# Computing adaLN modulation vectors: standing weight tiles on TensorE in one layer, row sums on VectorE in the other

## The chip, the cores and the metric

The kernel runs on one core of a Trainium2 chip. The metric is the device time in microseconds (us), and the lower the better; one execution was also recorded with the hardware profiler.

## The reference

Two trunk layers run over 256 context tokens and 1024 latent tokens of width 1024. Each layer has a mixing part (four kinds of two-direction chunked scans, then an output projection) and a channel part (a squared-ReLU MLP of width 4096). Both parts begin with a normalisation that is scaled and shifted by modulation vectors, and end in a residual addition with a gate. The change is in how these vectors are computed. Cut to that:

```
for layer in range(DEPTH):
    mod_l = silu(c) @ w_ada[layer] + b_ada[layer]        # latent tokens
    mod_c = silu(c_ctx) @ w_ada[layer] + b_ada[layer]    # context tokens
    sh1, sc1, g1, sh2, sc2, g2 = split(mod, 6)           # each 1024 long
    h = rmsnorm(x) * (1 + sc1) + sh1
    x = x + g1 * (mixers(h) @ w_out)
    h = rmsnorm(x) * (1 + sc2) + sh2
    x = x + g2 * (relu(h @ w1) ** 2 @ w2)
```

`w_ada` is 1024 x 6144 in each layer, 25 MB of 32-bit numbers. It is multiplied by two vectors only, one for the context and one for the latent tokens, so this is a matrix-vector product that sits beside large matrix products. The 6144 columns are cut into three thirds of 2048, numbered r = 0, 1, 2: the first holds sh1 and sc1, the second g1 and sh2, the third sc2 and g2.

## The kernel before, in words

Activations lie with features on the 128 partitions and tokens along the row, in token blocks of 256, 512 and 512. Every large product runs in a split precision: each operand is held as a high and a low part, and `mm3` (L293, L294, L295) issues three matmuls for one 128 x 128 block of weights. `whalf` loads 256 KB of raw weights on the SyncE queue (L280), makes the high part on ScalarE (L281) and the low part on VectorE (L282).

The program runs in this order for each layer: the mixers, the output projection, the MLP. The first third of the first layer's modulation (`ada_unit`) comes ahead of everything. The order on each engine is that of the Python program, rearranged at build time by a scheduler of the framework; on the chip each engine works through its list in that order and waits at an instruction that isn't ready.

**Mixers.** Scan work comes from generators (`mix_vec` and others), which put small matmuls on TensorE with VectorE and ScalarE work between them: L990 prepares operands on VectorE for the matmuls of L1018, L955 multiplies with two moving columns, L1043 copies on ScalarE what L833 multiplies. Dense projections are put between them as filler by the class `Fill`. A step of it is six matmuls of `mm3`, so that a projection of 128 columns over one token block has four steps; then an evacuation function reads the PSUM bank (L741 and others on VectorE). Dense blocks take their PSUM banks from a ring of three, `self.dbanks = Ring((0, 1, 2))`.

`Fill.also` is a second generator, advanced at some of the filler's steps. In the first layer it computes thirds 1 and 2 of that layer's modulation, by `ada_part` with pieces of W = 256 columns. For each of eight blocks of 128 rows, `ada_part` loads a tile (L402), multiplies it by the block's element of c for each of the two tokens and adds it to an accumulator (L406 for the first block, L408 for the others). After the eighth, a matmul with one column of ones (L413) sums each 128 columns of the accumulator over the partitions, and L419 adds the bias:

```
for k in range(NK):
    w = wring.next()(W)
    nc.sync.dma_start(w, self.io["w_ada"][l, r, k, :, g, h:h + W])
    for i, j in enumerate(toks):
        c = self.cc[:, k, j:j + 1]
        ...
            nc.vector.scalar_tensor_tensor(A[i], w, c, A[i], op0=ALU.mult, op1=ALU.add)
    yield
...
        nc.tensor.matmul(ps[...], lhsT=A[i][:, 128 * cb:128 * cb + 128], rhs=one, ...)
```

That is 144 yields in the first layer, at three of five steps. About 250 steps of the filler are left when `also` is set.

**MLP of the first layer.** The second layer's modulation is computed here, by the same `ada_part` with W = 512: third 0 for both tokens, thirds 1 and 2 for the latent token alone. The function `filler` advances it after each of the 32 blocks of hidden features. PSUM banks come from a ring of eight; L525 adds the output to the residual on VectorE, reading PSUM.

The matmuls of the modulation have plain 32-bit operands, and TensorE runs each of them as two instructions.

Of the kernel before, what the change touches and what calls it, by code (L numbers as in the profile page):

```python
# [156 lines left out]
class Fill:  # L157
# [10 lines left out]
    def step(self):  # L168
        while self.q:
# [3 lines left out]
            for cost in gen:  # L173
                self.n += 1
                if self.also and self.n % 5 in (0, 2, 4):
                    next(self.also, None)
                return cost
# [20 lines left out]
class K:  # L198
    def __init__(self, ctx, tc, io):
# [16 lines left out]
        self.d_a = dp.tile([2, 4, NC], F32, name="d_a")  # L216

# [98 lines left out]
    def params(self, tmp):  # L316
# [5 lines left out]
        nc.vector.tensor_tensor(c2, c2, b, op=ALU.mult)  # L322

# [67 lines left out]
    def ada_part(self, l, r, toks, wring, tmp, acc, banks, W):  # L391
# [3 lines left out]
        one = self.m64[:, 1:2]  # L395
        nt, nb = len(toks), W // 128
        for q in range(2048 // W):
            g, h = divmod(q * W, 512)
            A = [b(W) for b in acc[:nt]]
            for k in range(NK):  # L400
                w = wring.next()(W)
                nc.sync.dma_start(w, self.io["w_ada"][l, r, k, :, g, h:h + W])  # L402
                for i, j in enumerate(toks):
                    c = self.cc[:, k, j:j + 1]
                    if k == 0:
                        nc.vector.tensor_scalar(A[i], w, c, None, op0=ALU.mult)  # L406
                    else:
                        nc.vector.scalar_tensor_tensor(A[i], w, c, A[i], op0=ALU.mult, op1=ALU.add)  # L408
                yield
            ps = self.bank(banks().next())  # L410
            for i in range(nt):
                for cb in range(nb):
                    nc.tensor.matmul(ps[:, 2 * cb + i:2 * cb + i + 1], lhsT=A[i][:, 128 * cb:128 * cb + 128], rhs=one,  # L413
                                     start=True, stop=True)
            o = 16 * r + nb * q
            mo = self.mod[:, l, o:o + nb, toks[0]:toks[0] + nt]
            bb = self.bada[:, l, o:o + nb].unsqueeze(2).to_broadcast([128, nb, nt])
            v = ps[:, 0:2 * nb].rearrange("p (c j) -> p c j", j=2)[:, :, 0:nt]
            nc.vector.tensor_tensor(mo, v, bb, op=ALU.add)  # L419
            if (r == 0 and g >= 2) or (r == 2 and g < 2):  # L420
                nc.vector.tensor_scalar(mo, mo, 1.0, None, op0=ALU.add)
            yield
# [1315 lines left out]
```

## Time and profile before

| | |
|---|---|
| median of 3 timed runs | 3307.71 us (3307.68 to 3312.28) |
| the profiled execution's own time | 3300.05 us |
| its span, first to last instruction | 3298.2 us |
| TensorE (PE) busy | 3215.6 us, 97% |
| VectorE (DVE) busy | 2121.8 us, 64% |
| ScalarE (ACT) busy | 1286.1 us, 39% |
| mean granted TensorE clock | 0.992 of full speed |
| moved by DMA | 278.85 MB, 85 GB/s on the mean |

Stretches of the span are given in us from its start. The first layer's mixers end at about 790, its output projection at about 900, its MLP at about 1800; then the second layer follows. PE stands for TensorE's matmuls, PEld for its weight loads, DVE for VectorE, ACT for ScalarE, SP for SyncE. Busy time of a group is the union of its instructions where they overlap one another, and the mean is that of one instruction from start to end, so that a pipelined instruction costs less than its mean.

### The profile page before, as it was taken

The page shows a single profiled execution, that of the slowest core. Times are in us where ns is not written, and L with a number is a line of the kernel's source. Part 1 is how long each engine was busy: PE and PEld are TensorE (multiplying, and loading weights), DVE is VectorE, ACT ScalarE, POOL GpSimd, SP SyncE. Part 2 cuts the span into 40 slices and gives each one's busy share as a digit, 9 for nine tenths or more (in the row PEclk, how much of TensorE's full clock was granted, in tenths as well). Part 3 has the DMA queues.
Part 4 walks back from the last instruction along what each step waited for, and adds up shares of the span by engine and source line. Part 5 has one row for each costly group of instructions (what it writes and reads, how often), then busy time and mean ns, then how long its engine had stood idle before and what let it go on. Part 6 is the DMA issues. An engine that isn't in the chain of part 4 may idle for free.

```text
span 3298.2 us, 52930 instructions
## 1 busy us (share of the span) xinstructions
PE 3215.6 (97%) x20936; PEld 2640.0 (80%) x20936; DVE 2121.8 (64%) x4218; ACT 1286.1 (39%) x2665; POOL 10.8 (0%) x41
## 2 busy tenths in 40 slices
PE   7998899999999999999999999999999999999998
PEld 4786688877888888888888678788778888888887
DVE  4778887787666656555655586866756555554546
ACT  4665565445322122121212565765445322222222
POOL 0000000000000000000000000000000000000000
PEclk9999899999999999999999999999999999999999
DMA  5113444434322222222211222333315111111111
GB/s 206 61 50 127 122 133 148 121 101 146 103 80 71 83 65 80 69 64 64 77 39 34 76 66 77 110 114 109 103 58 163 53 50 46 51 51 46 51 48 65
DMA packets 175010, 278.85 MB, mean 85 GB/s; under 512 B 21097, under 2 KB 66825, under 8 KB 174505
## 3 DMA queue, kind: packets, MB, share of 16 engines
q1 hardware_dynamic: 173464, 273.66, 26.5%
q8 instruction: 164, 2.69, 0.3%
q10 hardware_dynamic: 1296, 1.81, 0.2%
q14 instruction: 86, 0.70, 0.1%
HBM read 229.75 MB, written 45.64 MB: 83 GB/s over the span
## 4 chain that ended last, share of the span: by engine, by line
PE 88%; DVE 5%; DMA 3%; ACT 3%; issue 1%; SPq 0%; DVEq 0%; ACTq 0%
PE psum L293 23%; PE psum L294 23%; PE psum L295 23%; PE psum L830 2%; PE psum L600 2%; PE psum L631 2%; PE psum L633 2%; PE psum L632 1%; PE psum L817 1%; PE psum L833 1%; PE psum L1018 1%; PE psum L705 1%; PE psum L1357 1%; PE psum L413 1%; DVE px L990 1%
## 5 line engine op out<-in xcount | busy, mean ns | idle before, releaser
L525 DVE SCALAR_TENSOR_TENSOR x<-psum,st,x 128x512 f32<-128x512 f32 (+1 forms) x648 | 441.3, 690 | 213.2 <-PE psum L295 212.3
L281 ACT ACTIVATE pc<-st 128x512 fp32r<-128x512 f32 x256 | 161.2, 632 | 847.5 <-PE psum L294 808.7
L294 PE MATMUL psum<-pc,pc 128*128 128x512 f32 (+1 forms) x1296 | 475.9, 367 | 0.0
L293 PE MATMUL psum<-pc,pc 128*128 128x512 f32 (+1 forms) x1296 | 475.8, 367 | 0.0
L295 PE MATMUL psum<-pc,pc 128*128 128x512 f32 (+1 forms) x1296 | 473.8, 366 | 0.0
L293 PE MATMUL psum<-Hhi,pc 128*128 128x512 f32 (+1 forms) x1280 | 471.9, 369 | 1.7 <-ACT pc L281 1.5
L294 PE MATMUL psum<-Hlo,pc 128*128 128x512 f32 (+1 forms) x1280 | 471.9, 369 | 0.1
L295 PE MATMUL psum<-Hhi,pc 128*128 128x512 f32 (+1 forms) x1280 | 470.5, 368 | 0.0
L293 PE MATMUL psum<-Hhi,pw 128*128 128x512 f32 (+1 forms) x1192 | 451.0, 379 | 5.7 <-ACT pw L281 2.5
L295 PE MATMUL psum<-Hhi,pw 128*128 128x512 f32 (+1 forms) x1192 | 445.2, 374 | 0.0
L294 PE MATMUL psum<-Hlo,pw 128*128 128x512 f32 (+1 forms) x1192 | 444.8, 373 | 0.0
L504 DVE TENSOR_TENSOR st<-st 128x256 f32<-128x256 f32 (+1 forms) x160 | 101.8, 637 | 301.8 <-ACT pc L503 300.7
L293 PEld LDWEIGHTS psum<-pc,pc 128*128 128x128 f32 x1296 | 244.4, 189 | 43.8 <-DVE x L525 1.3
L295 PEld LDWEIGHTS psum<-pc,pc 128*128 128x128 f32 x1296 | 244.0, 188 | 43.0 <-issue 2.7
L294 PEld LDWEIGHTS psum<-pc,pc 128*128 128x128 f32 x1296 | 244.5, 189 | 41.3 <-issue 2.1
L293 PEld LDWEIGHTS psum<-Hhi,pc 128*128 128x128 f32 x1280 | 241.2, 189 | 43.5 <-ACT pc L281 2.4
L294 PEld LDWEIGHTS psum<-Hlo,pc 128*128 128x128 f32 x1280 | 241.3, 189 | 40.9 <-DVE Hlo L481 0.5
L295 PEld LDWEIGHTS psum<-Hhi,pc 128*128 128x128 f32 x1280 | 241.1, 188 | 40.9 <-DVE pc L282 0.6
L293 PEld LDWEIGHTS psum<-Hhi,pw 128*128 128x128 f32 x1192 | 226.7, 190 | 51.4 <-issue 10.1
L282 DVE TENSOR_TENSOR pc<-st,pc 128x512 fp32r<-128x512 f32 x256 | 175.5, 690 | 137.9 <-ACT pc L281 117.3
L295 PEld LDWEIGHTS psum<-Hhi,pw 128*128 128x128 f32 x1192 | 226.2, 190 | 37.6 <-issue 2.1
L294 PEld LDWEIGHTS psum<-Hlo,pw 128*128 128x128 f32 x1192 | 226.8, 190 | 36.2 <-issue 2.2
(398 smaller groups left out, 4950.4 us busy)
## 6 DMA issues: line engine op xcount, KB each, us to landing
st<-w_ff SPq DMA_DIRECT2D x256, 256.0 KB
st<-w_inT SPq DMA_DIRECT2D x96, 256.0 KB
ph<-w_ada SPq DMA_DIRECT2D x128, 128.0 KB
st<-w_out SPq DMA_DIRECT2D x50, 256.0 KB
pc<-w_ada SPq DMA_DIRECT2D x48, 256.0 KB
st<-w_ada SPq DMA_DIRECT2D x48, 256.0 KB
d_z<-st SPq DMA_DIRECT2D x40, 256.0 KB
ps<-w_ada SPq DMA_DIRECT2D x32, 256.0 KB
```

The lines of the kernel that those rows point to most:

```text
L281: nc.scalar.activation(hi, raw, AF.Copy)
L282: (eng or nc.vector).tensor_tensor(lo, raw, F(hi), op=ALU.subtract)
L293: t.matmul(out, lhsT=w[0], rhs=m[0], start=first, stop=False)
L294: t.matmul(out, lhsT=w[0], rhs=m[1], start=False, stop=False)
L295: t.matmul(out, lhsT=w[1], rhs=m[0], start=False, stop=last)
L413: nc.tensor.matmul(ps[:, 2 * cb + i:2 * cb + i + 1], lhsT=A[i][:, 128 * cb:128 * cb + 128], rhs=one, start=True, stop=True)
L504: nc.vector.tensor_tensor(r, r, r, op=ALU.mult)
L525: nc.vector.scalar_tensor_tensor(x, ps, self.mod[:, l, 40 + o, j:j + 1], x, op0=ALU.mult, op1=ALU.add)
L600: t.matmul(ps[:, 0:304], lhsT=h[a], rhs=u[b], start=(k + i == 0), stop=(k == NK - 1 and i == 2))
L631: t.matmul(ps[:, e, :], lhsT=h[0], rhs=u[0], start=(k == 0), stop=False)
L633: t.matmul(ps[:, e, :], lhsT=h[1], rhs=u[0], start=False, stop=(k == NK - 1))
L830: nc.tensor.matmul(o, lhsT=ST[r0:r0 + kd, c, d, :], rhs=qd[d](c)[r0:r0 + kd, :], start=(j == 0), stop=False, tile_position=(r0, 0))
```

## The change

First layer, thirds 1 and 2 (`ada_tiles`): for each of the 32 blocks of 128 output columns, eight 128 x 128 blocks of `w_ada` are loaded as two tiles of 512 words, each block stands as TensorE's weights, and the two tokens' c are the two moving columns. The eight products add up in PSUM, and one VectorE instruction adds the bias. Three tile buffers replace four tiles and two accumulators; the generator is advanced at every seventh step of the filler.

Second layer (`ada_rows`): the weights are stored transposed, so that an output column's 1024 weights lie along a row. A half row of c is loaded into all 128 partitions (from a copy in device memory, `d_c`, written at the start on GpSimd's queue), and one VectorE instruction multiplies a 128 x 512 tile with it and sums each row. The two halves are added, then the bias. TensorE takes no part. The rows go through five buffers, c through one; `filler` advances it by three yields of two tiles each. For third 0 the tiles are loaded once for each token.

The arrays of weights are laid out on the host for this: `w_adaW` for the first layer, `w_adaR` for the second.

```
--- before.py
+++ after.py
@@ -172,7 +172,7 @@
                 self.q[1].pre(self.slots - self.q[0].n)
             for cost in gen:
                 self.n += 1
-                if self.also and self.n % 5 in (0, 2, 4):
+                if self.also and self.n % 7 == 0:
                     next(self.also, None)
                 return cost
             self.q.pop(0)
@@ -214,6 +214,7 @@
         self.d_b = dp.tile([4, 128, NT], F32, name="d_b")
         self.d_v = dp.tile([128, NC, 260], F32, name="d_v")
         self.d_a = dp.tile([2, 4, NC], F32, name="d_a")
+        self.d_c = dp.tile([2, 1024], F32, name="d_c")
 
 
     @staticmethod
@@ -320,6 +321,8 @@
         self.logsig(b, c2, a)
         nc.scalar.activation(b, b, AF.Exp)
         nc.vector.tensor_tensor(c2, c2, b, op=ALU.mult)
+        for j in range(2):
+            nc.gpsimd.dma_start(self.d_c[j].rearrange("(k p) -> p k", p=128), self.cc[:, :, j])
 
     def params2(self, tmp):
@@ -388,36 +391,43 @@
             m = self.mod[:, l, a:a + 8, :]
             nc.vector.tensor_scalar(m, m, 1.0, None, op0=ALU.add)
 
-    def ada_part(self, l, r, toks, wring, tmp, acc, banks, W):
-
-
-        nc = self.nc
-        one = self.m64[:, 1:2]
-        nt, nb = len(toks), W // 128
-        for q in range(2048 // W):
-            g, h = divmod(q * W, 512)
-            A = [b(W) for b in acc[:nt]]
-            for k in range(NK):
-                w = wring.next()(W)
-                nc.sync.dma_start(w, self.io["w_ada"][l, r, k, :, g, h:h + W])
-                for i, j in enumerate(toks):
-                    c = self.cc[:, k, j:j + 1]
-                    if k == 0:
-                        nc.vector.tensor_scalar(A[i], w, c, None, op0=ALU.mult)
-                    else:
-                        nc.vector.scalar_tensor_tensor(A[i], w, c, A[i], op0=ALU.mult, op1=ALU.add)
+    def ada_tiles(self, l, rs, wring, banks, queue):
+
+
+        nc = self.nc
+        for r in rs:
+            for o in range(16):
+                ps = self.bank(banks().next())[:, 0:2]
+                for h in range(2):
+                    w = wring.next()(4, 128)
+                    queue.dma_start(w, self.io["w_adaW"][r - rs[0], o, :, 4 * h:4 * h + 4, :])
+                    for k in range(4):
+                        nc.tensor.matmul(ps, lhsT=w[:, k, :], rhs=self.cc[:, 4 * h + k, 0:2], start=(h + k == 0), stop=(h * k == 3))
+                c = 16 * r + o
+                one = 1.0 if r == 2 and o < 8 else 0.0
+                nc.vector.tensor_scalar(self.mod[:, l, c, :], ps, self.bada[:, l, c:c + 1], one, op0=ALU.add, op1=ALU.add)
                 yield
-            ps = self.bank(banks().next())
-            for i in range(nt):
-                for cb in range(nb):
-                    nc.tensor.matmul(ps[:, 2 * cb + i:2 * cb + i + 1], lhsT=A[i][:, 128 * cb:128 * cb + 128], rhs=one,
-                                     start=True, stop=True)
-            o = 16 * r + nb * q
-            mo = self.mod[:, l, o:o + nb, toks[0]:toks[0] + nt]
-            bb = self.bada[:, l, o:o + nb].unsqueeze(2).to_broadcast([128, nb, nt])
-            v = ps[:, 0:2 * nb].rearrange("p (c j) -> p c j", j=2)[:, :, 0:nt]
-            nc.vector.tensor_tensor(mo, v, bb, op=ALU.add)
-            if (r == 0 and g >= 2) or (r == 2 and g < 2):
+
+    def ada_rows(self, l, r, toks, wring, cs, queue):
+
+
+        nc = self.nc
+        S = self.mod[:, 1 - l, 0:16, :]
+        for j in toks:
+            for h in range(2):
+                c = cs.next()(512)
+                queue.dma_start(c, self.d_c[j:j + 1, 512 * h:512 * h + 512].to_broadcast([128, 512]))
+                for o in range(16):
+                    w = wring.next()(512)
+                    queue.dma_start(w, self.io["w_adaR"][r, o, :, 512 * h:512 * h + 512])
+                    nc.vector.scalar_tensor_tensor(w, w, 1.0, c, op0=ALU.mult, op1=ALU.mult, accum_out=S[:, o:o + 1, h])
+                    if o % 2:
+                        yield
+            mo = self.mod[:, l, 16 * r:16 * r + 16, j]
+            nc.vector.tensor_tensor(mo, S[:, :, 0], S[:, :, 1], op=ALU.add)
+            nc.vector.tensor_tensor(mo, mo, self.bada[:, l, 16 * r:16 * r + 16], op=ALU.add)
+            if r in (0, 2):
+                mo = self.mod[:, l, 16 * r + (8 if r == 0 else 0):16 * r + (16 if r == 0 else 8), j]
                 nc.vector.tensor_scalar(mo, mo, 1.0, None, op0=ALU.add)
             yield
@@ -1455,7 +1465,7 @@
 
         ao = hp.alloc(1536, True) if l == 0 else None
         if l == 0:
-            fill.also = ada([ao.sub(256 * i, 256) for i in range(6)], lambda: self.dbanks)
+            fill.also = ada([ao.sub(512 * i, 512) for i in range(3)])
         self.feat_hg(hg[0])
         share(hg[0], hg[1], "V")
         fill.add(*(self.gate(6 + p, GLG + p, True) for p in range(2)))
@@ -1591,9 +1601,8 @@
         tbs = TBS if l == 0 else TBS[1:]
         b.mix_open(l)
 
-        def ada(bufs, banks):
-            for r in (1, 2):
-                yield from b.ada_part(0, r, (0, 1), Ring(bufs[:4]), None, bufs[4:6], banks, 256)
+        def ada(bufs):
+            return b.ada_tiles(0, (1, 2), Ring(bufs), lambda: b.dbanks, nc.sync)
         b.mixers(l, ada)
         b.outproj(l)
         na = 3
@@ -1604,12 +1613,12 @@
         aring = Ring(zip(cs[nw + nf::2], cs[nw + nf + 1::2]))
         def ada1(bufs, l=l):
             for r in range(3) if l == 0 else ():
-                yield from b.ada_part(1, r, (0, 1) if r == 0 else (1,), Ring(bufs[:4]), None, bufs[4:6], lambda: b.banks, 512)
+                yield from b.ada_rows(1, r, (0, 1) if r == 0 else (1,), Ring(bufs[:5]), Ring(bufs[5:]), nc.sync)
         tmps = b.tmps
         gen = ada1(cs[nw:nw + nf] + tmps.items[4:])
 
         def filler():
-            for _ in range(4):
+            for _ in range(3):
                 next(gen, None)
         if l == 0:
             b.tmps = Ring(tmps.items[:4])
@@ -1705,7 +1714,9 @@
     for d in range(2):
         ga[:, 16 * d:16 * d + 16, d, :] = gla_w_a[:, d]
     A["gla_w"] = ga
-    A["w_ada"] = ca(w_ada.reshape(2, 8, 128, 3, 4, 512).transpose(0, 3, 1, 2, 4, 5))
+    A["w_ada"] = ca(w_ada[:1, :, :2048].reshape(1, 8, 128, 1, 4, 512).transpose(0, 3, 1, 2, 4, 5))
+    A["w_adaW"] = ca(w_ada[0, :, 2048:].reshape(8, 128, 2, 16, 128).transpose(2, 3, 1, 0, 4))
+    A["w_adaR"] = ca(w_ada[1].T.reshape(3, 16, 128, 1024))
     at = _cols()
     seg = lambda n: w_in[:, :, at[n][0]:at[n][1]]
     iff = seg("ml_if").reshape(2, 1024, 2, 2, 4)
```

## Rows read from the trace of the kernel before

**Rows 1.** Busy table of the page: busy us, share of the span, instructions.

```profile
span 3298.2 us, 52930 instructions
...
PE 3215.6 (97%) x20936; PEld 2640.0 (80%) x20936; DVE 2121.8 (64%) x4218; ACT 1286.1 (39%) x2665; POOL 10.8 (0%) x41
```

**Rows 2.** Chain that ended last, of the page: shares by engine.

```profile
PE 88%; DVE 5%; DMA 3%; ACT 3%; issue 1%; SPq 0%; DVEq 0%; ACTq 0%
```

**Rows 3.** Windows: stretch, length, busy PE, PEld, DVE, ACT, POOL; granted clock, DMA.

```profile
250.00:300.00 50.00, 47.15 (x401) 34.94 (x400) 38.27 (x114) 34.60 (x96) 0.00 (x0) 1.00 0.45 143
300.00:400.00 100.00, 77.96 (x738) 61.90 (x737) 84.78 (x193) 57.08 (x111) 0.00 (x0) 0.85 0.36 111
400.00:800.00 400.00, 396.83 (x3221) 325.95 (x3220) 319.50 (x827) 198.92 (x497) 1.53 (x14) 1.00 0.40 120
1000.00:1700.00 700.00, 700.00 (x3703) 604.15 (x3702) 410.10 (x673) 144.32 (x254) 0.00 (x0) 1.00 0.23 70
1950.00:2450.00 500.00, 491.32 (x4562) 397.78 (x4560) 361.15 (x818) 292.56 (x661) 1.60 (x14) 1.00 0.31 97
```

**Rows 4.** Windows, finer, the stretches with a granted clock below 1.

```profile
310.00:330.00 20.00, 10.66 (x126) 8.64 (x127) 17.40 (x40) 7.41 (x14) 0.00 (x0) 0.66 0.26 86
360.00:400.00 40.00, 34.85 (x303) 28.31 (x304) 30.74 (x74) 20.49 (x41) 0.00 (x0) 0.79 0.46 139
```

**Rows 5.** Waits of PE, 290 to 790: total us, times, longest.

```profile
PE psum L1018 <- DVE px L990: 9.8, 4, 4.6
PE psum L833 <- ACT px L1043: 5.5, 4, 3.0
PE psum L413 <- DVE ph L408: 3.5, 1, 3.5
PE psum L293 <- DVE st L741: 2.3, 1, 2.3
```

**Rows 6.** Line L413: count, ns min/median/max, first and last start, by layer.

```profile
L413 PE MATMUL psum<-st,ph x128: 164/250/353, 292.9 to 763.1; 128*128 128x1 f32 x128
...
L413 PE MATMUL psum<-st x128: 164/250/250, 1005.2 to 1682.3; 128*128 128x1 f32 x128
```

**Rows 7.** Timeline of PE around one burst: start, us, instruction.

```profile
1005.21 1.84 PE L413 MATMUL psum<-st 128*128 128x1 f32 x16
1006.91 0.37 PE L293 MATMUL psum<-Hhi,pc 128*128 128x256 f32 x1
1007.12 0.28 PE L294 MATMUL psum<-Hlo,pc 128*128 128x256 f32 x1
1007.24 0.28 PE L295 MATMUL psum<-Hhi,pc 128*128 128x256 f32 x1
```

**Rows 8.** Timeline of PE around matmuls with two moving columns.

```profile
335.40 0.95 PE L955 MATMUL psum<-st,px 128*128 128x2 f32 x8
336.21 0.48 PE L295 MATMUL psum<-Hhi,pw 128*128 128x512 f32 x1
336.52 0.39 PE L293 MATMUL psum<-Hhi,pw 128*128 128x512 f32 x1
336.75 0.40 PE L294 MATMUL psum<-Hlo,pw 128*128 128x512 f32 x1
```

**Rows 9.** DVE groups, 216 to 790, then 900 to 1750: busy us, mean ns.

```profile
L408 DVE SCALAR_TENSOR_TENSOR ph<-ph,st 128x256 f32<-128x256 f32 x224 | 99.7, 479 | 0.2 <-DMA ph<-w_ada 0.2
...
L406 DVE TENSOR_SCALAR ph<-ph,st 128x256 f32<-128x256 f32 x32 | 10.7, 347 | 4.2 <-PE psum L413 4.2
...
L408 DVE SCALAR_TENSOR_TENSOR st<-st 128x512 f32<-128x512 f32 x64 | 46.8, 747 | 3.0 <-DMA st<-w_ada 2.9
```

**Rows 10.** Line L419: count, ns min/median/max, first and last start.

```profile
L419 DVE TENSOR_TENSOR st<-psum,st x28: 156/164/171, 295.3 to 1682.5; 128x4 f32<-128x4 f32 x24, 128x8 f32<-128x8 f32 x4
```

**Rows 11.** Windows of line L408, then of L406, 300 to 400.

```profile
300.00:400.00 100.00, 17.92 (x40) 0.85 0.36 111
...
300.00:400.00 100.00, 1.22 (x4) 0.85 0.36 111
```

**Rows 12.** DMA queue, 100 to 110: packets, MB, share of 16 engines.

```profile
q1 hardware_dynamic: 110, 0.00, 0.6%
```

## The prediction

> **What bounds the kernel now.** I read the busy table first: TensorE is busy for 3215.6 of 3298.2 us [rows 1], so the reader should see an engine with 83 us of idle time in the whole span. Busy time alone proves little, so next comes the chain of work that ended last: 88% of it is TensorE, 5% VectorE [rows 2]. A change can thus gain in two ways only: less TensorE work, or fewer of those idle microseconds.
>
> The windows view says where they lie [rows 3]. In the first layer's MLP (1000 to 1700 us) TensorE is busy for all 700 us; VectorE does the second layer's modulation there at 410 of 700, and nothing waits for it. In the first layer's mixers TensorE idles for 2.9 us in 250 to 300, 22.0 us in 300 to 400 and 3.2 us in 400 to 800: 28.1 us together. In the second of these VectorE is busy for 85%, and the granted clock is 0.85. Cut finer [rows 4], the clock falls to 0.66 and 0.79 just where TensorE has been idle. The clock has two levels, 2.4 and 1.2 GHz, so a mean c says that 2(1-c) of the time ran at half speed, and a busy time b holds about (1-c)b lost: 0.34 x 10.7 + 0.21 x 34.9 = 10.9 us, an estimate. What the mixers lose is so about 28 + 11 = 39 us. The waits view names the releasers: VectorE (L990, L413's own accumulators, L741) and one ScalarE copy [rows 5].
>
> The second layer's mixers run the same code without modulation work. From 1950 to 2450 they idle for 8.7 us in 500 at full clock with VectorE at 72% [rows 3]. That is the yardstick for the first layer once VectorE is relieved.
>
> **The change, part by part.**
>
> *TensorE's added work.* A matmul with 32-bit operands runs as two records: 64 of L413 in each layer show as 128 [rows 6]. The price of a burst comes from the starts around it. Sixteen records with one moving column start at 1005.21; the second matmul after them starts at 1007.12; 0.12 of that is the ordinary step of the 256-column matmuls: 1.79 us, 0.111 a record, change of operand type included [rows 7]. Two moving columns are not dearer: eight records of L955 take 336.52 - 335.40 - 0.23 = 0.89 us, again 0.111 [rows 8]. The weights are what costs. Added: 2 thirds x 16 columns x 8 blocks = 256 matmuls, 512 records, 56.8 us, as 32 bursts of 1.78 us. Removed: 128 records in the first layer, 14.2 us, and 128 in the second layer's part, 14.2 us. TensorE's account: +56.8 - 28.4 = +28.4 us. The 14.2 us of the MLP are a sure gain, as that stage has no idle time to hide them; the mixers get +42.6.
>
> Here a page of the Trainium skill can be weighed. The row shows 0.111 us for a record with one or two columns. "TensorE: Matmul & The Clock Gate", section "Back-to-back issue gap", gives some 60 cycles for an isolated matmul of 1 to 64 columns, about 25 ns at full clock. By that figure the account would be 256 x 0.025 = +6.4 us in place of +28.4; the measurement decides, and it goes with the weight loads.
>
> *VectorE's relief in the mixers.* Gone are 224 multiply-adds, 99.7 us, and 32 multiplies, 10.7 us [rows 9]; the 16 additions of bias become 32 at 0.16 us [rows 10], 2.6 us more. In 300 to 400 the relief is 17.9 + 1.2 = 19.1 us [rows 11] of the 84.8.
>
> *How much of the 39 us comes back.* In 300 to 400 TensorE's own work without waits and slow clock is 78.0 - 10.9 = 67.1; less 24 old records (2.7) it is 64.4. The old bursts lie between 292.9 and 763.1 [rows 6] with 15 steps of the filler to each (9 yields at 3 of 5); that makes about 2.1 us a step, so 7 steps are 14.6 us: 6.8 bursts in this stretch, 12.1 us, and TensorE needs 76.5. VectorE then has 84.8 - 19.1 + 1 = 67. So VectorE stops being the longer of the two. Bounds: nothing comes back if the gaps are latency alone; all 33 (22.0 + 10.9) comes back if TensorE simply becomes the limit. I leave 8 of it: the 5.5 us behind the ScalarE copies of L1043 [rows 5], which VectorE's load does not make, and about 2 us per 100 as in the second layer. So 25 come back here. Of the 6 us in the other stretches I count 1. Together 26 us, bounds 15 and 39.
>
> *VectorE in the MLP.* 112 multiply-adds and 16 multiplies of 512 elements become 128 row sums of 512 elements. The multiply-add costs 747 ns [rows 9]; no row shows one that also sums along its row. Between 0.75 and twice that, VectorE gains between about 6 and 102 us of work in a stage where it idles for 290 of 700, and TensorE never waits [rows 3]. I cost it at nothing. The cover is that idle time and the ring of eight banks; if it were gone, the weight splits behind it (L282) would be late.
>
> *Transfers.* In the mixers 128 loads of 128 KB become 64 of 256 KB, the same bytes. A tile's buffer is freed at least one burst, some 15 us, before its next use, so its load is early; but now it is TensorE, in order, and not VectorE that stands behind a late one, with the dense work queued behind. In the MLP 96 loads become 128, with 8 loads of a repeated half row of c through one buffer: the SyncE queue waits there for sixteen sums, and the weight loads behind it wait too; with TensorE at no idle in 700 us I count nothing. The two stores of c at the start are 2048 elements of 4 bytes on GpSimd's queue, while the DMA engines feed the start. The nearest row: 110 tiny packets take 0.6% of 16 engines' 10 us, 8.7 ns each [rows 12]; 2048 of them over 16 engines are 1.1 us. Bounds 0 and 3; I take +1.
>
> *Sum.* +28.4 - 26 + 1 = +3.4 us. Against the profiled execution: span 3298.2 to 3301.6, time 3300.05 to 3303.5. The median of the timed runs, 3307.71, lies 7.7 above that execution; I put the same 3.4 on it: 3311.1.
>
> **The rivals.**
>
> *The gaps are latency (slower).* VectorE's work is mixed finely with the scan's, and the chain from ScalarE to VectorE to TensorE may be long whatever the load. Then only about 15 to 18 of the 39 return: 28.4 - 16.5 + 1 = +13, 3321. For it: L1018's waits for L990 are single waits of up to 4.6 us [rows 5]. Against it: the second layer runs that chain at 8.7 us in 500. It decides from the point where less than 23 us return.
>
> *Banks of the filler (slower).* The dense work and the bursts share a ring of three PSUM banks. A burst every 7 steps and a dense block of 4 steps mean that nearly every third turn is a burst's, so that dense work alternates between two banks and must wait until VectorE has read the one before. A wait of this kind is in the trace once, 2.3 us (L293 for L741) [rows 5]. At a third of the 32 bursts it is 25 us on top of the sum: +28, 3336. It decides from three such waits on. Against it: a freer VectorE reads sooner.
>
> *All comes back (faster).* The bursts fall into TensorE's gaps and the clock stays up: 28.4 + 1 - 38 = -8.6, 3299. It needs 36 of 39 us; a stretch as clean as 400 to 800, at 3.2 us in 400 [rows 3], speaks for it.
>
> *The page's issue gap holds (faster).* If the weight loads of consecutive bursts hid each other, the account would be +6.4 and the sum 6.4 - 26 + 1 = -18.6, 3289. The rows measure 0.111 with the same operand shapes, so I give it under 1 in 50.
>
> *Row sums hold up the MLP (slower).* The 14.2 us are given back: +18, 3326. TensorE's 700 of 700 speaks against it.
>
> **How the numbers follow.** The forecast (22 to 35 us return, nothing new waits) has 0.45 and reaches from -5.6 to +7.4 us, 3302 to 3315. Latency 0.23, banks 0.11, row sums 0.04: slower together 0.38. All back 0.15 and the issue gap 0.02: faster 0.17. A measurement of this kernel tells about 0.2%, 6.6 us, from no change; the cases fall on these bounds nearly as they stand. The time is that of the forecast, 3311. The range takes in the rival with everything back (3299) and the latency rival with some waits at the banks, to +20 (3328).
>
> **What would show it.** Right: 512 records of the new matmul line between about 220 and 760 us at 0.111 each; VectorE near 67 of 100 in the stretch from 300, the clock back near 1.00 there, idle time of TensorE in 250 to 800 under 12 us; the first layer's mixers ending some 17 us later (42.6 - 26), its MLP 14 us shorter, everything after the same. Wrong: slow clock still there in 300 to 400; new waits of L293 for VectorE's readers or of the burst for its tile; an MLP no shorter. The likeliest mistake is the 26 us: it is a judgement between 15 and 39, and each microsecond of it counts one to one.

## The result, and the profile after

| | median us | runs | against the kernel before |
|---|---|---|---|
| before | 3307.69 | 4 (3304.78 to 3312.28) | |
| changed | 3345.91 | 4 (3340.27 to 3353.0) | ratio 1.0115, 95% interval 1.009 to 1.014 |

The change costs 38 us; 3311 was forecast, with 3328 as the upper end. The profiled execution of the changed kernel took 3340.27 us (span 3338.5), so it is 40.2 us slower than the one of before. In the changed kernel lines have new numbers: `mm3` is now L294, L295, L296, the tiles' matmuls are L405, the row sums L423, and L1018, L990, L525 are now L1028, L1000, L535.

The busy table and the chain of waits tell little: TensorE has 47.6 us more busy time than in [rows 1], VectorE 90 us less, and the chain is TensorE's as in [rows 2].

```profile
PE 3263.2 (98%) x21192; PEld 2684.3 (80%) x21192; DVE 2032.0 (61%) x4097; ACT 1285.3 (39%) x2665; POOL 12.7 (0%) x43
PE 86%; DVE 6%; DMA 4%; ACT 3%; issue 1%; SPq 0%; DVEq 0%; ACTq 0%
```

So I look first at where the time is lost. Two lines that the change doesn't touch serve as marks: the first scan matmul of the first layer's mixers, and the third matmul of the MLP's first product, whose first and last starts bracket that MLP. Of the kernel before (count, duration in ns, first and last start in us, shapes):

```profile
L1018 PE MATMUL psum<-px x1216: 213/219/317, 152.3 to 512.3; 128*32 128x64 f32 x91, 64*32 64x64 f32 x83
L295 PE MATMUL psum<-Hhi,pc x768: 274/389/397, 934.9 to 1806.5; 128*128 128x512 f32 x129, 128*128 128x256 f32 x63
```

The same marks in the changed kernel:

```profile
L1028 PE MATMUL psum<-px x1216: 213/219/244, 161.5 to 535.2; 128*32 128x64 f32 x91, 64*32 64x64 f32 x83
L296 PE MATMUL psum<-Hhi,pc x768: 277/389/397, 975.9 to 1840.9; 128*128 128x512 f32 x129, 128*128 128x256 f32 x63
```

| stretch | from the marks | forecast |
|---|---|---|
| start, to the first scan matmul | 161.5 - 152.3 = +9.2 | +1 |
| first layer's mixers and output projection | 975.9 - 934.9 - 9.2 = +31.8 | +16.6 |
| first layer's MLP | 865.0 - 871.6 = -6.6 | -14.2 |
| the rest, to the end of the span | 40.3 - 34.4 = +5.9 | 0 |

**The start.** Windows of 5 us of the changed kernel (length; busy us and instructions of TensorE, weight load, VectorE, ScalarE, GpSimd; clock; DMA share; GB/s):

```profile
20.00:25.00 5.00, 2.47 (x6) 0.28 (x4) 0.00 (x0) 0.00 (x0) 0.00 (x0) 0.99 1.70 105
25.00:30.00 5.00, 1.92 (x2) 0.18 (x2) 0.00 (x0) 0.00 (x0) 0.00 (x0) 0.50 0.81 119
```

and the queues of its first 60 us (packets, MB, share of the 16 DMA engines) show what is there beside the loads:

```profile
q0 software_dynamic: 64, 0.01, 4.1%
```

The two d_c stores are 64 packets on GpSimd's queue. 4.1% of 16 engines' 60 us is 39 us: 615 ns a packet. While they pass, the loads of the first weights fall to 105 and 119 GB/s, and TensorE waits and drops to its lower clock (0.50). How 39 us, spread over 16 engines, hold the loads back for 10 us is not shown.

**The mixers.** The windows that answer to [rows 3], and three short ones:

```profile
250.00:300.00 50.00, 46.95 (x387) 36.92 (x386) 33.30 (x95) 26.04 (x68) 0.00 (x0) 0.91 0.50 160
300.00:400.00 100.00, 97.04 (x907) 81.14 (x906) 70.77 (x155) 62.48 (x133) 0.00 (x0) 0.94 0.36 115
400.00:800.00 400.00, 398.07 (x3275) 333.50 (x3274) 239.08 (x608) 184.90 (x463) 1.53 (x14) 0.98 0.35 110
...
634.00:646.00 12.00, 12.00 (x78) 9.37 (x78) 4.94 (x16) 3.58 (x13) 0.00 (x0) 0.86 0.43 129
646.00:658.00 12.00, 12.00 (x86) 9.11 (x85) 6.92 (x22) 4.67 (x11) 0.00 (x0) 0.99 0.28 85
658.00:672.00 14.00, 14.00 (x87) 12.74 (x86) 8.50 (x22) 6.35 (x16) 0.00 (x0) 0.76 0.39 120
```

Idle time fell from 28.1 to 3.1 + 3.0 + 1.9 = 7.9 us, under the 12 of the forecast. The clock did not come up. By the prediction's own formula, (1-c) of the busy time, 0.09 x 46.95 + 0.06 x 97.04 + 0.02 x 398.07 = 18.0 us go to it, against 10.9. And it now falls also where TensorE isn't idle at all by this profile: 0.86 and 0.76 at 12.00 of 12.00 and 14.00 of 14.00 us. The timeline says what TensorE did before that (start, us, engine, line, tiles, shape, count):

```profile
656.45 1.45 PE L1367 MATMUL psum<-ph,px 128*128 128x65 f32 x12
657.70 0.48 PE L295 MATMUL psum<-Hlo,pw 128*128 128x512 f32 x1
...
660.96 1.84 PE L405 MATMUL psum<-st,ph 128*128 128x2 f32 x16
662.66 0.37 PE L294 MATMUL psum<-Hhi,pw 128*128 128x256 f32 x1
662.87 2.33 PE L1367 MATMUL psum<-ph,px 128*128 128x65 f32 x12
664.95 0.56 PE L295 MATMUL psum<-Hlo,pw 128*128 128x256 f32 x1
665.31 0.41 PE L296 MATMUL psum<-Hhi,pw 128*128 128x256 f32 x1
665.52 0.41 PE L294 MATMUL psum<-Hhi,pw 128*128 128x256 f32 x1
665.74 0.41 PE L295 MATMUL psum<-Hlo,pw 128*128 128x256 f32 x1
```

The burst itself takes 1.70 us from start to start, close to its forecast price of 1.78. Behind it twelve matmuls of L1367 take 2.1 us, where the same twelve took 1.25 us at 656.45, and the matmuls of 256 columns start 0.21 us apart where [rows 7] shows 0.12: half speed, with no gap. The 0.86 lies around a burst at 640.

**The MLP.** The row sums' first and last starts, and what TensorE and VectorE waited for there:

```profile
L423 DVE SCALAR_TENSOR_TENSOR st<-st x74: 675/682/694, 993.5 to 1173.8; 128x512 f32<-128x512 f32 x74
L423 DVE SCALAR_TENSOR_TENSOR pc<-pc,st x54: 675/682/695, 978.1 to 1175.1; 128x512 f32<-128x512 f32 x54
```
```profile
PE psum L295 <- DVE pc L515: 5.5, 1, 5.5
...
DVE pc L423 <- DMA st<-d_c: 11.3, 5, 4.2
```

All 128 sums run within 197 us. The Python order spreads them over 23 blocks, but they depend on nothing in the MLP and they come together in the scheduler's order. In that rush VectorE, in order, waits for their operands with the block's own subtraction (L515) behind it; once, near 1117, TensorE waits 5.5 us for it and then runs in part at the lower clock (0.66 in 1120 to 1130, at 7.87 us busy). By the formula the two are 5.5 + 0.34 x 7.87 = 8.2 us; by the marks 7.6 of the 14.2 were given back.

### The profile page after: what moved, and what is told of

It is laid out like the page before. It is cut to its first block, busy times and chain, and to the rows that moved or that the text cites. A ratio compares the mean times of both kernels' runs of the same rounds, so it can differ in the third digit from the quotient of the medians.

```text
span 3338.5 us, 53238 instructions
## 1 busy us (share of the span) xinstructions
PE 3263.2 (98%) x21192; PEld 2684.3 (80%) x21192; DVE 2032.0 (61%) x4097; ACT 1285.3 (39%) x2665; POOL 12.7 (0%) x43
## 4 chain that ended last, share of the span: by engine, by line
PE 86%; DVE 6%; DMA 4%; ACT 3%; issue 1%; SPq 0%; DVEq 0%; ACTq 0%
PE psum L294 22%; PE psum L296 22%; PE psum L295 22%; PE psum L840 2%; PE psum L405 2%; PE psum L610 2%; PE psum L641 2%; PE psum L643 1%; PE psum L642 1%; PE psum L827 1%; PE psum L843 1%; PE psum L1028 1%; PE psum L1367 1%; PE psum L715 1%; DMA ps<-w_ada 1%
## 5 line engine op out<-in xcount | busy, mean ns | idle before, releaser
L535 DVE SCALAR_TENSOR_TENSOR x<-psum,st,x 128x512 f32<-128x512 f32 (+1 forms) x648 | 440.7, 689 | 204.8 <-PE psum L296 204.2
L295 PE MATMUL psum<-pc,pc 128*128 128x512 f32 (+1 forms) x1296 | 477.2, 368 | 5.5 <-DVE pc L515 5.5
L294 PE MATMUL psum<-pc,pc 128*128 128x512 f32 (+1 forms) x1296 | 476.5, 368 | 0.0
L296 PE MATMUL psum<-pc,pc 128*128 128x512 f32 (+1 forms) x1296 | 475.1, 367 | 0.0
L294 PE MATMUL psum<-Hhi,pc 128*128 128x512 f32 (+1 forms) x1280 | 471.1, 368 | 1.8 <-ACT pc L282 1.8
L295 PE MATMUL psum<-Hlo,pc 128*128 128x512 f32 (+1 forms) x1280 | 472.0, 369 | 0.1
L296 PE MATMUL psum<-Hhi,pc 128*128 128x512 f32 (+1 forms) x1280 | 470.5, 368 | 0.0
L294 PE MATMUL psum<-Hhi,pw 128*128 128x512 f32 (+1 forms) x1192 | 456.6, 383 | 0.5 <-ACT ph L769 0.3
L296 PE MATMUL psum<-Hhi,pw 128*128 128x512 f32 (+1 forms) x1192 | 450.2, 378 | 0.0
L295 PE MATMUL psum<-Hlo,pw 128*128 128x512 f32 (+1 forms) x1192 | 446.1, 374 | 0.0
L295 PEld LDWEIGHTS psum<-pc,pc 128*128 128x128 f32 x1296 | 245.3, 189 | 47.6 <-DVE pc L515 6.0
L294 PEld LDWEIGHTS psum<-pc,pc 128*128 128x128 f32 x1296 | 245.1, 189 | 44.1 <-DVE x L535 1.2
L296 PEld LDWEIGHTS psum<-pc,pc 128*128 128x128 f32 x1296 | 244.8, 189 | 43.0 <-issue 2.7
L294 PEld LDWEIGHTS psum<-Hhi,pc 128*128 128x128 f32 x1280 | 241.3, 189 | 43.6 <-ACT pc L282 2.7
L295 PEld LDWEIGHTS psum<-Hlo,pc 128*128 128x128 f32 x1280 | 241.3, 189 | 41.0 <-issue 0.5
L296 PEld LDWEIGHTS psum<-Hhi,pc 128*128 128x128 f32 x1280 | 241.2, 188 | 40.9 <-DVE pc L283 0.6
L283 DVE TENSOR_TENSOR pc<-st,pc 128x512 fp32r<-128x512 f32 x256 | 175.6, 689 | 154.9 <-ACT pc L282 135.1
L294 PEld LDWEIGHTS psum<-Hhi,pw 128*128 128x128 f32 x1192 | 229.0, 192 | 45.6 <-issue 9.9
L296 PEld LDWEIGHTS psum<-Hhi,pw 128*128 128x128 f32 x1192 | 228.9, 192 | 39.3 <-issue 2.4
L295 PEld LDWEIGHTS psum<-Hlo,pw 128*128 128x128 f32 x1192 | 229.2, 192 | 35.6 <-issue 1.7
```

Of the source, the lines that this page charges most:

```text
L283: (eng or nc.vector).tensor_tensor(lo, raw, F(hi), op=ALU.subtract)
L294: t.matmul(out, lhsT=w[0], rhs=m[0], start=first, stop=False)
L295: t.matmul(out, lhsT=w[0], rhs=m[1], start=False, stop=False)
L296: t.matmul(out, lhsT=w[1], rhs=m[0], start=False, stop=last)
L535: nc.vector.scalar_tensor_tensor(x, ps, self.mod[:, l, 40 + o, j:j + 1], x, op0=ALU.mult, op1=ALU.add)
```

## The experiments

Each ran in five rounds against the kernel before, whose median was 3306.8, 3308.7 and 3310.7 us in the three sessions (E1 to E4, E5 to E8, E9 to E12).

| run | median us | ratio, 95% interval |
|---|---|---|
| E1 tiles only | 3336.95 | 1.0089 (1.0072 to 1.0106) |
| E2 rows only | 3313.19 | 1.0014 (1.0000 to 1.0028) |
| E3 changed, store in runs | 3337.54 | 1.0085 (1.0066 to 1.0104) |
| E4 changed, two buffers for c | 3347.22 | 1.0122 (1.0105 to 1.0140) |
| E5 tiles only, sums left out | 3256.50 | 0.9842 (0.9825 to 0.9859) |
| E6 tiles only, bursts of 8 | 3349.01 | 1.0118 (1.0100 to 1.0136) |
| E7 tiles only, bursts of 4 | 3386.66 | 1.0229 (1.0208 to 1.0249) |
| E8 tiles only, 32 columns | 3318.41 | 1.0028 (1.0016 to 1.0040) |
| E9 changed, 32 columns and runs | 3315.20 | 1.0013 (1.0000 to 1.0027) |
| E10 as E9, rows paced | 3305.75 | 0.9981 (0.9968 to 0.9995) |
| E11 rows only, runs, paced | 3296.34 | 0.9953 (0.9938 to 0.9969) |
| E12 as E11, mixers' sums on GpSimd | 3405.42 | 1.0282 (1.0262 to 1.0301) |

**E1 and E2, one part alone.** The first layer by `ada_tiles` with the second as before (no d_c), and the reverse.

> First layer by standing tiles on TensorE, second layer as in the kernel before, no d_c and so no d_c stores. Theory (three separate losses: start +9 by the d_c stores, mixers +31 by the bursts, MLP one stall of 8 against 14 saved): the mixers' +31 alone, 3339 us against 3307.7 before, with the start as before (nothing lost by 60 us) and the low clock again in stretches of the mixers where TensorE is busy throughout. Rival A, the delay at the start is what throws the mixers' clock and schedule off: without the stores the mixers lose only the 17 us of the forecast, 3325. Rival B, the loss lies in the second layer's part: 3308.

> First layer as in the kernel before, second layer by row sums, with the d_c stores at the start. Theory: start +9, mixers as before, MLP -14 by the records of L413 that are gone and +8 by the wait for the copies of c, so about +3: 3311 us against 3307.7. Rival, that start delay is covered by later idle time: 3302. Rival, the row sums themselves hold up the MLP: over 3315.

E1 costs 30.1 us, E2 6.4: together 36.5 of the 38.2. The first scan matmul starts at 152.1 in E1 and at 159.9 in E2, so the start's loss goes with the d_c stores; without it the mixers of E1 lose no less (its MLP starts at 972.3: 972.3 - 934.9 + 0.2 = +37.6; by the medians E1 costs 30.1 in all). Both of E1's rivals fall. E2's MLP is 6.6 us shorter, as in the changed kernel.

**E3, the store in runs.**

```
-        for j in range(2):
-            nc.gpsimd.dma_start(self.d_c[j].rearrange("(k p) -> p k", p=128), self.cc[:, :, j])
+        cj = tmp.sub(0, 16)(2, 8)
+        nc.vector.tensor_copy(cj, self.cc[:, :, 0:2].rearrange("p k j -> p j k"))
+        nc.gpsimd.dma_start(self.d_c.rearrange("j (p k) -> p j k", k=8), cj)
```

The second layer's weights are laid out in c's new order.

> The changed kernel, but c is first copied into runs of 8 and stored by one transfer of 32-byte runs, not two of 4-byte elements. Theory: the small packets took the 16 engines from the first weights, so the start's 9 us come back: 3337 us against 3346 for the changed kernel, and the lag at 60 us against the kernel before is under 2 us. Rival, it is the wait for c or the place of the store on its queue, not the packets: 3346 still.

8.4 us came back, by the medians. The same windows, and the queue:

```profile
20.00:25.00 5.00, 4.88 (x29) 1.49 (x26) 0.00 (x0) 1.45 (x4) 0.00 (x0) 1.00 1.05 392
25.00:30.00 5.00, 4.96 (x22) 1.26 (x20) 0.00 (x0) 1.28 (x3) 0.00 (x0) 1.00 1.04 380
```
```profile
q0 software_dynamic: 32, 0.01, 0.1%
```

Same bytes, same queue, same place: the runs are longer, one transfer stands for two, and 4.1% became 0.1%. The first scan matmul starts at 152.4 in place of 161.5, so the start's 9 us are back. The MLP of this profiled execution starts only 0.9 us earlier, at 975.0: its mixers took 8.2 us more than those of the changed kernel, with the same code; such scatter is in the table behind E8.

**E4, two buffers for c** (`Ring(bufs[:4]), Ring(bufs[4:])`).

> The changed kernel, but with four buffers for the rows of w and two for the copies of c, not five and one. Theory: the load of the next half of c no longer stands behind the last sum of the half before, VectorE's waits for it (17.9 us in 7) go, and with them TensorE's idle time of 5.5 us and its slow clock near 1120 us: 3338 us against 3346, with the MLP 14 us shorter than in the kernel before. Rival, the waits are those for the rows of w, which have one buffer less here: no change or slower, 3346 to 3350.

My theory fell: no gain. VectorE's waits for d_c went, those for the rows grew (the rows of w_adaR, 3.1 us in 8 waits in the changed kernel's sums on `st`, 8.8 in 10 here), and TensorE's wait stayed:

```profile
PE psum L295 <- DVE pc L515: 6.0, 1, 6.0
...
DVE st L423 <- DMA st<-w_adaR: 5.2, 7, 1.6
```

(The second row is of 1080 to 1140 us.) So the buffer of c was only the place where the rush happened to wait. E10 takes away the rush.

**E5, the bursts taken away.** The loop of loads and matmuls in `ada_tiles` goes; `tensor_scalar` reads `self.cc[:, 0, 0:2]` in place of `ps`.

> As the run with the first layer's tiles alone (3337 us), but the two thirds' loads and matmuls are left out: one entry of c and the bias stand in for the sum. No burst and no sum on VectorE in the first layer's mixers. Theory (VectorE's sums cause the idle time, the bursts cause the low clock): TensorE loses its 14.2 us of L413 and 22.5 us of idle time, and the low clock falls under the 9 us of before: 3307 - 14 - 23 - 4 = about 3266. Rival, the bursts only filled gaps that are there anyway, so that idle time stays near 30 us without them: 3307 - 14 = 3293. Rival, the low clock belongs to the mixers' own small matmuls: 3270 with as many slow stretches as with the bursts.

It took 3256.5, under the forecast. The windows:

```profile
250.00:300.00 50.00, 49.22 (x412) 36.60 (x410) 35.79 (x100) 35.99 (x99) 0.00 (x0) 1.00 0.43 136
300.00:400.00 100.00, 98.24 (x942) 78.42 (x940) 79.28 (x177) 64.46 (x133) 0.63 (x6) 1.00 0.33 108
400.00:800.00 400.00, 392.60 (x3132) 325.43 (x3132) 265.63 (x632) 214.19 (x521) 0.91 (x8) 1.00 0.35 112
```

The clock is 1.00 and 9.9 us of idle time are left, most of them past 400. Both rivals fall: the gaps of before came with the sums, not from the scan's own latency or from a lack of filler, and the first layer's mixers without bursts leave the clock up. E5 leaves out the loads too; E1 and E8, which keep them, idle for 8.1 and 6.7 us in these windows, so it was VectorE's work and not the loads that made the gaps. Sums at no price would be worth 52 us.

**E6 and E7, shorter bursts.** A step issues 8 (or 4) records into a bank of its own, and VectorE adds the parts; the filler takes a step at `n % 7 in (0, 3)` (or `(0, 2, 4, 5)`).

> The first layer's tiles alone, but each burst of 16 records is two bursts of 8 with a bank, a VectorE operation and a step of the filler of their own; 512 records as before, 32 VectorE operations more. Theory (a run of 16 small records in a row lowers the clock): the slow stretches that begin at a burst past 400 us are gone, as they were in the kernel before with its bursts of 4 and 8, and the clock there is 1.00: 3337 - 9 = 3328. Rival (it is the number of such records, however they lie): the slow stretches stay, 3337; with more banks and evictions in the filler, up to 3342.

> As the run with bursts of 8, cut once more: 128 bursts of 4 records, 96 VectorE operations more than with bursts of 16. Theory: no slow stretch that begins at a burst, 3326. Rival (number of records): 3337. Rival (each burst has a price of its own, by the change from one shape of matmul to another and by its bank): 3345 and more, with idle time in place of slow clock.

Both misses. E6 has no slow stretch past 600, but more before 400 (0.85 in 300 to 400, where TensorE is busy for 90.66 of 100 us); E7 loses 50 us against E1. Between the first scan matmul and the MLP, TensorE idles for 26.3 us in E6 and 42.9 in E7, against 14.2 in E1; it is busy for 799.8, 818.1 and 806.0. Part of E7's idle time is the prediction's rival of the filler's banks. E7's waits (225 to 860 us; L440 is the burst, L293 the dense work, L744 reads the bank before):

```profile
PE psum L440 <- DVE st L744: 5.0, 2, 3.2
PE psum L293 <- DVE st L744: 4.2, 2, 3.4
```

With two more rows of the burst, 2.5 us each, such waits are 14.2 us; the rest is spread over many other waits, none above 5.6 us in total. These two runs change the length of a burst, the number of bank turns and the order of everything around, so they don't tell whether a shorter burst alone would keep the clock up.

**E8, more columns, everything else as E1.**

```
-                ps = self.bank(banks().next())[:, 0:2]
+                ps = self.bank(banks().next())[:, 0:32]
...
-                        nc.tensor.matmul(ps, lhsT=w[:, k, :], rhs=self.cc[:, 4 * h + k, 0:2], ...)
+                        nc.tensor.matmul(ps, lhsT=w[:, k, :], rhs=self.cc[:, 4 * h + k, :], ...)
```

VectorE reads the first two columns of the result.

> The first layer's tiles alone, with 32 moving columns (two of c and thirty of no use) in place of two. Theory (a record costs the turn of its weights, 0.112 us, and the columns are hidden in it): a burst still costs 1.79 us; as the records move 16 times as many columns, the clock stays up and the time falls by some of the 8 us of slow clock: 3331. Rival A (the clock falls by the weights' turn, whatever moves): 3337. Rival B (columns count in the price): 32 columns at the price of a 65-column matmul of this kernel, 0.108 us, added to each record: 3337 + 25 = 3362.

Thirty useless columns a record save 18.5 us (20 if each run is taken against the kernel before of its own session). The windows and a burst:

```profile
250.00:300.00 50.00, 47.33 (x402) 36.65 (x401) 29.71 (x89) 29.39 (x81) 0.00 (x0) 0.97 0.51 161
300.00:400.00 100.00, 97.34 (x941) 79.64 (x940) 77.35 (x172) 64.57 (x132) 0.10 (x1) 1.00 0.41 131
400.00:800.00 400.00, 398.62 (x3329) 334.43 (x3328) 245.04 (x613) 187.81 (x467) 1.43 (x13) 1.00 0.34 107
```
```profile
656.21 1.87 PE L436 MATMUL psum<-st,ph 128*128 128x32 f32 x16
657.92 0.48 PE L293 MATMUL psum<-Hhi,pw 128*128 128x512 f32 x1
658.23 0.39 PE L294 MATMUL psum<-Hlo,pw 128*128 128x512 f32 x1
658.46 0.40 PE L295 MATMUL psum<-Hhi,pw 128*128 128x512 f32 x1
```

The burst takes 1.71 us, as with two columns, and 512 columns behind it start 0.23 us apart, full speed. The slow clock costs 0.03 x 47.33 = 1.4 us here and, by the same formula, 22.9 us in E1 (0.83, 0.97, 0.97 in these windows); idle time is alike, 6.7 and 8.1 us. Slow clock and idle time together, 8.1 in E8 and 31.0 in E1, account for 22.9 of the 24.2 us between the two profiles' MLP marks (948.1 and 972.3). So nearly all of the gain is the clock. The two profiled executions are E8's fastest and E1's slowest, but the clock separates all their runs: over the whole span it is 0.993 to 0.997 in E8's twelve and 0.987 to 0.991 in E1's six.

In E1, too, the clock falls behind bursts with no gap. Seven windows that begin at bursts between 385 and 687, 69 us in all, have TensorE busy for every microsecond and a clock of 0.69 to 0.83. One of them, and 500 us of E8 with bursts of the same length:

```profile
659.00:670.00 11.00, 11.00 (x75) 10.72 (x71) 5.43 (x13) 4.38 (x10) 0.00 (x0) 0.69 0.36 119
...
300.00:800.00 500.00, 495.96 (x4267) 414.07 (x4266) 322.39 (x784) 252.37 (x598) 1.53 (x14) 1.00 0.36 112
```

The stretch from the first scan matmul to the first MLP mark (mixers and output projection) can be compared in ten profiled executions. Those in one line run the same code there. First the window as the view gives it, of before, the changed kernel and E8:

```profile
152.30:934.90 782.60, 746.12 (x6344) 610.22 (x6344) 597.28 (x1440) 407.34 (x925) 1.53 (x14) 0.98 0.36 113
161.50:975.90 814.40, 799.91 (x6727) 664.95 (x6728) 511.79 (x1196) 406.46 (x925) 1.53 (x14) 0.97 0.34 109
153.30:948.10 794.80, 780.19 (x6727) 648.61 (x6728) 512.78 (x1196) 407.55 (x925) 1.53 (x14) 1.00 0.35 111
```

| first layer's mixers | length us | TensorE busy us | idle us |
|---|---|---|---|
| sums on VectorE: before, E2, E11 | 782.6, 788.4, 788.1 | 746.1, 753.8, 753.7 | 36.5, 34.6, 34.4 |
| bursts, 2 columns: changed, E1, E3, E4 | 814.4, 820.2, 822.6, 819.8 | 799.9, 806.0, 807.5, 805.0 | 14.5, 14.2, 15.1, 14.8 |
| bursts, 32 columns: E8, E9, E10 | 794.8, 796.3, 796.9 | 780.2, 781.4, 783.9 | 14.6, 14.9, 13.0 |

The second and third lines have equally many matmuls and the same idle time, but their ranges of busy time lie 16 us apart. What differs is the clock. The first line also shows that the profile of before was a favourable one: against E2 and E11 the bursts of two columns cost 26 to 35 us, not 32 to 40.

**E9 to E11, the mends together.** E9 is the changed kernel with E3's and E8's edits. E10 also ties each block's row sums to that block:

```
-                filler()
+                filler(r)
...
+                b.go = b.cc[:, fno[0] % 8, 2 + fno[0] // 8:3 + fno[0] // 8]
+                nc.vector.tensor_scalar(b.go, r[:, 0:1], 0.0, 1.0, op0=ALU.mult, op1=ALU.add)
...
-                    nc.vector.scalar_tensor_tensor(w, w, 1.0, c, ...)
+                    nc.vector.scalar_tensor_tensor(w, w, self.go, c, ...)
```

E11 has the first layer of before, and the second by rows with E3's store and E10's pacing.

> The changed kernel with both mends: 32 moving columns in the first layer's tiles and d_c stored in runs of 32 bytes. Theory: start +0, mixers +10 (as the run with 32 columns alone stood to the kernel before), MLP -14 and +8 for its stall: 3308 + 10 - 6 = 3312, which is where the forecast stood. Rival (the two losses overlap, or the clock falls for another reason with the second layer's rows there): 3325.

> As the run with both mends, but each block of the MLP writes a one from its own result (one VectorE operation of one column, 32 in all), and the row sums of that block take it as their scalar, so that no row sum can run ahead of its block. Theory (all 128 sums ran within 200 us because nothing held them back; VectorE and the queue of loads then hold up the block's own subtraction): the sums lie over 23 of the 32 blocks, no wait of TensorE for L515 of 5 us and no slow clock near 1120: 3312 - 8 = 3304. Rival (a sum that waits for its row stalls VectorE wherever it stands): 3312 or more, with such waits at other places. Rival (pacing makes each block's sums late and the next block waits): 3320.

> First layer as in the kernel before, second layer by row sums, paced by their blocks, with d_c stored in runs. Theory: only the 14.2 us of the MLP's records of L413 go, nothing is lost at the start or in the MLP: 3308 - 14 = 3294, under both kernels. Rival (the MLP's stall stays): 3302.

All three fell within 4 us of their theory. (E9's 3315 is near the forecast of 3311 by chance: its mixers cost less than the 16.6 of the forecast, and its MLP saves 5.4 and not 14.2.) Pacing is worth 9.5 us (3315.2 to 3305.75). In E10 the sums and the first 150 us of the MLP are:

```profile
L424 DVE SCALAR_TENSOR_TENSOR st<-st x74: 735/746/753, 972.3 to 1537.8; 128x512 f32<-128x512 f32 x74
...
1000.00:1150.00 150.00, 150.00 (x783) 129.04 (x782) 91.76 (x186) 32.81 (x58) 0.00 (x0) 1.00 0.29 92
```

TensorE is busy throughout, though VectorE still waits up to 5.2 us for c. The MLP's marks lie 856.8 us apart, 14.8 less than before: the 14.2 of the forecast, no longer given back. E10 is thereby 5 us under the kernel before, and E11 beats both kernels.

**E12, the mixers' sums on GpSimd.** `ada_part`'s two operations become products and additions of 512 elements on `nc.gpsimd`.

> As the run before, but the first layer's sums run on GpSimd (a product and an addition for both columns at a time, 256 operations of 128x512 in all), which is idle in the mixers; L413's small matmuls in the mixers stay. Theory (VectorE's share in these sums is what makes TensorE idle there): 23 of the 32 us of idle time and most of the 9 us of slow clock come back with no burst to pay: 3294 - 30 = 3264. Rival A (GpSimd needs over 2 us an operation and the first layer's output projection waits for it): 3294 + 30 and more. Rival B (GpSimd beside VectorE slows VectorE's operations): the mixers gain less, 3285.

The theory fell, by 109 us against E11. GpSimd needs 1.2 and 1.5 us an operation, 314 us in all, under the 2 of Rival A. But VectorE is slower beside it. Its 45 weight splits (L283) and its operands for the scan (L1015, in E11 L1018), in E12 and then in E11 (count; busy us, mean ns; idle):

```profile
L283 DVE TENSOR_TENSOR pw<-st,pw 128x512 fp32r<-128x512 f32 x45 | 44.2, 986 | 17.9 <-ACT pw L282 17.9
...
L1015 DVE SCALAR_TENSOR_TENSOR px<-px,st 128x512 f32<-128x512 f32 x40 | 43.8, 1095 | 3.7 <-ACT px L1013 3.0
```
```profile
L283 DVE TENSOR_TENSOR pw<-st,pw 128x512 fp32r<-128x512 f32 x45 | 30.4, 683 | 2.2 <-ACT pw L282 2.1
...
L1018 DVE SCALAR_TENSOR_TENSOR px<-px,st 128x512 f32<-128x512 f32 x40 | 29.8, 746 | 2.4 <-ACT px L1016 2.3
```

TensorE's longest wait in E12's mixers is for L1015, 26.5 us. Between the marks it idles for 99.4 us in place of E11's 34.4, and the same 6344 matmuls keep it busy for 792.4 in place of 753.7: 65 us of idle time and 39 of slow clock are 104 of the 109 us.

## Why the prediction was wrong

**TensorE's added work: right.** 512 records from 290 to 778 us, a burst at 1.70 us, two columns no dearer than one. Weight loads set the price; 32 columns don't change it.

**"How much of the 39 us comes back": this step failed.** It joined two things, some 15 us of idle time and the 10.9 of slow clock, into one recovery of 26 us, on the reading that the clock falls where TensorE has been idle [rows 4]. The idle part came back and more: VectorE stood at 70.8 in 300 to 400 (67 forecast), and 20.2 of the 28.1 us returned. The clock part did not: 10.9 us became 18.0. Net 13.1 came back, and the mixers cost 42.6 - 13.1 = 29.5 by these rows, 31.8 by the marks. E8 shows that the slow clock made the difference: with the clock up, 21.4 + 9.5 = 30.9 come back, and the mixers cost 11.7 by the rows and 948.1 - 934.9 - 1.0 = 12.2 by the marks, less than the forecast 16.6.

By how much the bursts made the clock worse than before is not settled. By the same formula the mixers of before lost 19.3 and 20.6 us to it in E2 and E11 (0.19 x 80.75 + 0.01 x 393.73, and 0.07 x 48.01 + 0.17 x 78.10 + 0.01 x 397.21); those with bursts of two columns lost 22.9, 26.7 and 22.9 in E1, E3 and E4. What is shown is that idle time went and slow clock stayed, and that it goes with 32 columns: 1.4, 1.4 and 5.2 us in E8, E9 and E10.

The Trainium skill, "TensorE: Matmul & The Clock Gate", section "HAM oscillation — how this bites in real kernels", has a rule of this kind: no idle gaps on TensorE, or the clock drops. The trace of before agrees [rows 4]; that of the changed kernel shows a fall that the rule doesn't cover, 0.76 at 14.00 us busy of 14.00. The measurement decides: in these mixers, bursts that move two columns behind full weight loads can cost the clock as gaps do. They need not do so elsewhere: the 128 records with one column in the MLP of before, in bursts of up to 16, left it at 1.00 among dense work [rows 3, rows 6, rows 7].

**The two stores of c: mis-sized.** Forecast +1, bounds 0 and 3; measured +9.2. The sum took 2048 packets at the price of tiny ones on another queue (8.7 ns [rows 12]); there were 64 at 615 ns each, and they held back the very loads on which the start depends. E1 and E3 show it from both sides.

**"VectorE in the MLP at nothing", and the spread of the sums.** The 14.2 us were there, and 7.6 of them were given back; one wait of TensorE and the slow clock behind it account for that. The cover that I named was idle time over 700 us; the sums used 197 us of it. I took the order of the Python program for the order on the chip. E10 and E11 show that spread sums cost nothing. The single buffer for c was a wait that the prediction names, and E4 shows that it wasn't the cause. The prediction's lower figure for VectorE, a gain of 6 us of work, was a slip: 128 sums at 0.75 x 747 ns are 71.7 us, less than the 83.7 of the multiply-adds that they replace. Nothing hung on it.

**The rivals.** Latency: as little came back as it says, but its reason is refuted by E5 and E8. Banks: no such wait in the changed kernel (only 0.2 us on L294), though E7 shows what it would be. Row sums hold up the MLP: the right mechanism at half its price, at 0.04. All comes back: 13.1 of 39 us did. Issue gap: a record took 1.70 / 16 = 0.106 us.

**Open.** The 5.9 us in the rest of the program. Its code is the same in all runs, and the profiled executions differ from before there by -1.7 (E7) to +11.3 us (E12). The same 9152 matmuls keep TensorE busy there for 1461.9 us in E7, 1464.2 in before, 1467.1 in the changed kernel and 1471.3 in E2, so part of it is clock. As the profiled execution of before was also 7.6 us under its median, this looks like scatter; it was not tested. Why the clock falls at some bursts and not at others is open too, as is the 31.8 us in the mixers beyond the 29.5 of the rows.

## What to carry to other kernels

Price a TensorE edit twice: for the time of its records and for what it does to the clock of the large matmuls behind them; where the weights set the price, try wider moving operands: here 32 columns cost no more than two and paid for themselves. Work without a dependency on its surroundings need not stay where the program puts it: spread it by a dependency, or cost it as one lump. A small store is sized by its packets and by what else the queues carry at that moment, not by its bytes.

## What the runs showed of the hardware

- 32 moving columns in place of 2 took the granted clock of the mixers from 0.83, 0.97, 0.97 to 0.97, 1.00, 1.00 in the three windows, at the same 1.7 us a burst.
- A transposing store of 4-byte elements on GpSimd's queue: 615 ns of a DMA engine for each of 64 packets, and the other loads down from 392 GB/s (E3) to 105 and 119.
- A row sum costs no more than the multiply-add did (747 ns for 512 elements [rows 9]): 682 ns with a constant as its scalar (changed kernel) and 746 with one read from a tile (E10), and 80 ns for a separate instruction that reads the accumulator.
- GpSimd beside VectorE (E12): 45 operations with two inputs went from 683 to 986 ns, 40 others from 746 to 1095. The Trainium skill, "SBUF — State Buffer", section "SBUF: two separate sides", says that the two share a pair of ports which one holds for a whole instruction while the other waits; the trace agrees in direction, and the means here are 1.44 and 1.47 times.
